# Second-half queries projected beside the first attention and kept in DRAM, in a two-layer hybrid decoder trunk

## The chip, the cores and the metric

The kernel runs on one core of one Trainium2 chip. The metric is the device time of one execution in microseconds, as the median over several runs. All data that the kernel multiplies is float32; each weight and each activation is split into a high part and a remainder, and a product takes three matmuls (high by high, high by low, low by high).

## The reference, cut to what matters

```python
# x: (1, 1024, 1024); layer 0: RG-LRU mixer + MLP; layer 1: sparse attention + MLP
h = rmsnorm(x, norm_mix_g[i]) * (1.0 + sc1) + sh1          # adaLN
# layer 1, token mixer
u = h @ w_in                                               # q, k, v, index q, index k, index weight
q, k, v, qi, ki, wi = jnp.split(u, B_SPLITS, axis=-1)
q = apply_rope(rmsnorm(q.reshape(B, S, 16, 64), q_g), cos, sin)
k = apply_rope(rmsnorm(k, k_g)[:, :, None, :], cos, sin)[:, :, 0]
...
score = einsum("bqh,bqhs->bqs", wib, relu(logits))         # causal, top 256 keys of each query
p = softmax(where(valid, einsum("bqhd,bqkd->bqhk", qb, kg) * 64 ** -0.5, -inf))
out = einsum("bqhk,bqkd->bqhd", p, vg)                     # 16 heads share one key and one value
x = x + g1 * (out @ w_out)
h = rmsnorm(x, norm_ffn_g[i]) * (1.0 + sc2) + sh2
x = x + g2 * (square(relu(h @ ffn_w1[i])) @ ffn_w2[i])
```

## The kernel before, in words

The 1024 positions are two halves of 512. An activation is held as eight tiles of 128 features by 512 positions, so a projection of one half is a run of 128x512 matmuls. Tiles of this size come from one pool of 54 (`tile`, `tileR`); weights pass through `weights`, which loads 512 KB from SP's queue, casts the high part on ScalarE (L322) and subtracts the remainder on GpSimd or VectorE (L328), whose turn is set by the list `lo`. A scheduler decides the final order of the instructions on each engine and their waits.

Layer 1 runs in these stages. First the projections of the first half are made: keys, values and index parts (`kv_steps`, `qi_steps`) and the queries in two groups of 512 columns (`q_group(0, 0)` and `q_group(0, 1)`). A query group is 96 matmuls (L941 to L943), then, for each of four blocks of 128 positions, a root mean square per head, a rotation (`rope`, L804 to L807), a split into high part and remainder (`split_heads`, L859 and L860) and two turns of four 128x128 blocks on TensorE (`turn4`, L868, copied out by ScalarE at L873).

Then comes `attention(0)`, the attention of the first half. It goes through 16 units (a block of positions, a group, a parity), each of four heads: scores on TensorE (L1118, L1119), mask and row minimum on VectorE (L1130), the exponential on ScalarE (L1136), the scaling by the reciprocal sum on GpSimd (L1141), and then per block of keys a transpose (L1146), a copy and a remainder (L1148, L1149) and two matmuls with the values (L1158, L1159). While it runs, `mix` takes pieces from a generator `background()`, at a `rate` of pieces per call: in the first attention the keys, values and index parts of the second half (L819 to L821 by way of `proj_tok`), then the output projection of the first half's group 0 (L345 to L347, added at L1221), which has to wait until nine units are done. `feed` holds back the turns of a step until two later steps are under way.

After it the output projection of group 1, the index scores and the top-k search of the second half, and the MLP of the first half follow (`FFN.single`). Near the end of that MLP the queries of the second half are made. For this the kernel loads the residual `x` of the second half from DRAM (`reload(1)`, L1234), makes the normed input again (`Norm.apply`, L96 to L98; the first one, `hm[1]`, lives only until the first attention) and runs `q_group(1, 0)` and `q_group(1, 1)`, with two of the eight output blocks of the last piece of the MLP between them. Then `attention(1)` runs, with the other six output blocks as the first of its background. Scaling on GpSimd there works on rows of 640 to 1024 elements.

The functions that the change touches, with what calls them:

Of the kernel before, what the change touches and what calls it, by code (L numbers as in the profile page):

```python
# [9 lines left out]
FT = mybir.dt.float32  # L10
# [3 lines left out]
AF = mybir.ActivationFunctionType  # L14
OP = mybir.AluOpType
AX = mybir.AxisListType
# [4 lines left out]
HT = 512  # L21
P = 128
# [3 lines left out]
EPS = 1e-6  # L26
# [21 lines left out]
class Norm:  # L48


    def __init__(self, T, h):
        self.T, self.h = T, h
# [12 lines left out]
    def stat(self, sums=None):  # L65

        T, nc = self.T, self.T.nc
        if sums is None:
            sums = T.ps()[:, 0:4]
            for c in range(4):  # L70
                nc.tensor.matmul(sums[:, c:c + 1], self.acc[:, c * P:(c + 1) * P], T.ones[:, 0:1],
                                 start=True, stop=True)
        r = T.small([P, 4], "rs")
        nc.vector.tensor_scalar(r, sums, 1.0 / D, EPS, op0=OP.mult, op1=OP.add)
        r2 = T.small([P, 4], "rs")
        nc.gpsimd.tensor_tensor(r2, r, T.mhalf, op=OP.pow)
        self.dg = T.nlong()
        for c in range(4):
            nc.vector.tensor_scalar(self.dg[:, c * P:(c + 1) * P], T.ident, r2[:, c:c + 1], None, op0=OP.mult)  # L79
# [117 lines left out]
class Trunk:  # L197
    def __init__(self, ctx, tc, ins, out):
        self.ctx, self.tc, self.nc = ctx, tc, tc.nc
        self.n = 0  # L200
        self.i, self.out = ins, out
        nc = self.nc
        self.const = ctx.enter_context(tc.tile_pool(name="const", bufs=1))
        self.wp = ctx.enter_context(tc.tile_pool(name="wp", bufs=5))
        self.smp = ctx.enter_context(tc.tile_pool(name="smp", bufs=6))
        self.np = ctx.enter_context(tc.tile_pool(name="np", bufs=3))
        self.act = ctx.enter_context(tc.tile_pool(name="act", bufs=54))
        self.pst = ctx.enter_context(ExitStack())
        self.banks(False)
        self.dram = ctx.enter_context(tc.tile_pool(name="dram", bufs=1, space=bass.MemoryType.DRAM))  # L210
        self.tp = None
        self.x, self.xd = {}, {}
        self.parts, self.late = {}, []
        self.fill = []
        self.bg, self.rate, self.due = None, 1, 0.0
        self.lo, self.npump = [1], 1
        self.ada_late, self.loads = [], []
        self.ident = self.const.tile([P, P], FT, name="ident")
        make_identity(nc, self.ident)
        self.identR = self.const.tile([P, P], FR, name="identR")  # L220
        nc.vector.tensor_copy(self.identR, self.ident)
        self.ones = self.const.tile([P, P], FT, name="ones")
        nc.vector.memset(self.ones, 1.0)
        self.mhalf = self.const.tile([P, 4], FT, name="mhalf")
        nc.vector.memset(self.mhalf, -0.5)


# [700 lines left out]
    def q_group(self, h, g, hx, turns):  # L928
# [27 lines left out]
        for t in range(4):  # L956
# [13 lines left out]
            turns.append([lambda p=p, turn=turn: turn(p) for p in range(2)])  # L970
            yield

    def idx_steps(self, t):
        nc, V, A = self.nc, self.nc.vector, self.nc.scalar
        L = (t + 1) * P
# [276 lines left out]
    def run(self):  # L1252
        tc = self.tc
        mod = self.mod = {}
        N = {}
        hm, hf = {}, {}
# [11 lines left out]
        turns = []  # L1268
# [5 lines left out]
        def run(gen):  # L1274
            for _ in gen:
                pass

        def feed(fs, lag=2):
            for f in fs:
                turns.append((yield from f()))  # L1280
                while len(turns) > lag:
                    turn_next()
                yield
# [24 lines left out]
        F = FFN(self, 0, None, hf)  # L1308
        with ExitStack() as st:
# [42 lines left out]
            f2 = F.f2_steps([0], 0)  # L1352
# [23 lines left out]
        with ExitStack() as st:  # L1376
# [47 lines left out]
            def background():  # L1424
                self.second_half()
                yield from feed(self.kv_steps(1, hm[1]), 2)
                yield from feed(self.qi_steps(1, hm[1]), 2)
                self.reload(0)
                while self.units < 8 + 1:
                    yield  # L1430
                yield from self.proj_out(0, mod[1, 2], 0)

            self.banks(True)
            self.bg, self.rate = background(), 1
            self.attention(0)
            self.finish()
            flush()
        with ExitStack() as st:
# [26 lines left out]
            self.lo, self.npump = [1, 1, 0], 2  # L1465
            F = FFN(self, 1, mod[1, 5], hf)
            F.single(0, 0, F.NP - 2)
            self.reload(1)
            hm[2] = N["m1", 1].apply(mod[1, 1], mod[1, 0])
            self.lo = [1, 0]  # L1470
            run(self.q_group(1, 0, hm[2], turns))
            for p in (F.NP - 2, F.NP - 1):
                F.load2(p, 0)
            f2 = F.f2_steps([F.NP - 2, F.NP - 1], 0)
            next(f2), next(f2)
            run(self.q_group(1, 1, hm[2], self.late_turns))
            self.lo = [1]

            def before(u):
                t = u[0]  # L1480
                while len(self.fill) > 36 * (7 - t):
                    self.pump()

            for p in (F.NP - 2, F.NP - 1):
                F.load2(p, 1)

            def background():
                yield from f2
# [4 lines left out]
                yield from self.proj_out(1, mod[1, 2], 0)  # L1493

            self.bg, self.rate = background(), 0.8
            self.banks(False)
            self.attention(1, before)
            self.finish()
            run(self.proj_out(1, mod[1, 2], 1, sqs("f1")))
# [50 lines left out]
```

## Time and profile before

| | us |
|---|---|
| median of 3 runs | 2551.33 |
| lowest, highest | 2551.26, 2557.24 |
| the profiled execution | 2558.93 |
| its span, first to last instruction | 2557.0 |
| TensorE busy in the span | 2435.1 |
| first attention (before its output projection of group 1) | 1333 to 1483 |
| second query stage, to the first scores of the last attention | 1883.7 to 1958.8 |

The profiled execution is 7.6 us over the median of the runs. Its own time is 1.9 us more than its span. A profile lists busy times of each engine: TensorE's matmuls (PE), its weight loads (PEld), VectorE (DVE), ScalarE (ACT), GpSimd (POOL); SP issues most of the transfers. The end of a matmul is modelled: in a row of back-to-back 128x512 matmuls each is listed with some 0.39 us, while one starts every 0.233 us. So a busy share of TensorE says where it stood still, and not how dense the work was.

### The profile page before, as it was taken

The page shows a single profiled execution, that of the slowest core. Times are in us where ns is not written, and L with a number is a line of the kernel's source. Part 1 is how long each engine was busy: PE and PEld are TensorE (multiplying, and loading weights), DVE is VectorE, ACT ScalarE, POOL GpSimd, SP SyncE. Part 2 cuts the span into 40 slices and gives each one's busy share as a digit, 9 for nine tenths or more (in the row PEclk, how much of TensorE's full clock was granted, in tenths as well). Part 3 has the DMA queues.
Part 4 walks back from the last instruction along what each step waited for, and adds up shares of the span by engine and source line. Part 5 has one row for each costly group of instructions (what it writes and reads, how often), then busy time and mean ns, then how long its engine had stood idle before and what let it go on. Part 6 is the DMA issues. An engine that isn't in the chain of part 4 may idle for free. (4 is left out here: it accounts for less than half of the span.)

```text
span 2557.0 us, 30862 instructions
## 1 busy us (share of the span) xinstructions
PE 2435.1 (95%) x10954; PEld 1965.4 (77%) x10954; DVE 1502.1 (59%) x2905; ACT 1227.8 (48%) x2180; POOL 797.6 (31%) x507
## 2 busy tenths in 40 slices
PE   7998999999999999999987999999998999999999
PEld 6776787777788888788776777888887777788887
DVE  5888775788643412566677876555558875321212
ACT  3656465521211233235456667768634974423322
POOL 1000000022221243230238822322326994334442
PEclk8999999999999999999998999999999999999999
DMA  8564675356311577654321522322330114323231
GB/s 262 194 226 167 208 238 188 99 178 222 126 42 42 178 276 269 217 192 177 136 87 42 189 67 67 107 74 91 106 125 1 34 42 140 107 91 99 86 104 58
DMA packets 212284, 342.52 MB, mean 134 GB/s; under 512 B 19658, under 2 KB 123298, under 8 KB 212130
## 3 DMA queue, kind: packets, MB, share of 16 engines
q1 hardware_dynamic: 183184, 295.29, 34.2%
q10 hardware_dynamic: 28946, 45.27, 5.4%
q8 instruction: 86, 1.41, 0.2%
q14 instruction: 68, 0.56, 0.1%
HBM read 274.97 MB, written 65.54 MB: 133 GB/s over the span
## 5 line engine op out<-in xcount | busy, mean ns | idle before, releaser
L328 POOL TENSOR_TENSOR wl<-raw,wh 128x1024 fp32r<-128x1024 f32 (+2 forms) x194 | 470.7, 2433 | 1186.2 <-ACT wh L322 1169.3
L322 ACT CAST wh<-raw 128x1024 fp32r<-128x1024 f32 (+2 forms) x296 | 305.1, 1033 | 615.3 <-PE ps L346 238.8
L345 PE MATMUL ps<-a,wh 128*128 128x512 f32 x1152 | 461.0, 403 | 15.2 <-DVE a L723 7.5
L346 PE MATMUL ps<-a,wh 128*128 128x512 f32 x1152 | 459.2, 399 | 1.5 <-POOL a L1173 1.2
L347 PE MATMUL ps<-a,wl 128*128 128x512 f32 x1152 | 458.2, 399 | 0.7 <-DMA wl<-part 0.7
L345 PE MATMUL pd<-a,wh 128*128 128x512 f32 x1072 | 431.2, 404 | 12.2 <-DVE xc L636 9.4
L347 PE MATMUL pd<-a,wl 128*128 128x512 f32 x1072 | 429.5, 401 | 10.2 <-DVE wl L328 10.2
L346 PE MATMUL pd<-a,wh 128*128 128x512 f32 x1072 | 430.2, 402 | 2.0 <-DVE a L98 2.0
L168 DVE SCALAR_TENSOR_TENSOR a<-ps,mod,a 128x512 f32<-128x512 f32 x352 | 259.7, 746 | 262.8 <-PE ps L347 262.1
L345 PEld LDWEIGHTS ps<-a,wh 128*128 128x128 f32 x1152 | 218.5, 190 | 71.1 <-DVE a L723 7.9
L347 PEld LDWEIGHTS ps<-a,wl 128*128 128x128 f32 x1152 | 218.3, 190 | 54.4 <-DMA wl<-part 1.8
L346 PEld LDWEIGHTS ps<-a,wh 128*128 128x128 f32 x1152 | 218.4, 190 | 54.0 <-POOL a L1173 2.3
L345 PEld LDWEIGHTS pd<-a,wh 128*128 128x128 f32 x1072 | 204.6, 191 | 63.2 <-issue 6.5
L347 PEld LDWEIGHTS pd<-a,wl 128*128 128x128 f32 x1072 | 204.8, 191 | 60.7 <-DVE wl L328 11.1
L346 PEld LDWEIGHTS pd<-a,wh 128*128 128x128 f32 x1072 | 205.3, 191 | 53.2 <-DVE a L98 3.4
L1141 POOL TENSOR_SCALAR s<-s,rr 128x128 f32<-128x128 f32 (+7 forms) x128 | 225.9, 1782 | 35.8 <-DVE rr L1139 25.2
L345 PE MATMUL ps<-hid,wh 128*128 128x512 f32 x512 | 204.9, 400 | 9.6 <-DVE a L168 6.8
L346 PE MATMUL ps<-hid,wh 128*128 128x512 f32 x512 | 203.6, 398 | 0.0
L347 PE MATMUL ps<-hid,wl 128*128 128x512 f32 x512 | 203.6, 398 | 0.0
L1019 ACT ACTIVATE signs<-sc,tc 128x384 int8<-128x384 f32 (+5 forms) x186 | 164.0, 882 | 77.3 <-DVE tc L1034 66.0
L452 DVE SCALAR_TENSOR_TENSOR a<-a,cond,a 128x512 f32<-128x512 f32 x140 | 113.5, 840 | 40.7 <-DMA a<-in_ada_w_dram 40.3
L146 DVE TENSOR_TENSOR a<-r,a 128x512 fp32r<-128x512 f32 x64 | 46.8, 754 | 141.7 <-ACT a L145 140.4
(271 smaller groups left out, 3684.1 us busy)
## 6 DMA issues: line engine op xcount, KB each, us to landing
raw<-in_ffn_w_dram SPq DMA_DIRECT2D x192, 512.0 KB, 3.7
a<-in_ada_w_dram ACTq DMA_DIRECT2D x160, 256.0 KB, 3.4
part<-wl SPq DMA_DIRECT2D x69, 512.0 KB, 3.2
wl<-part SPq DMA_DIRECT2D x69, 512.0 KB, 4.3
part<-wh SPq DMA_DIRECT2D x40, 512.0 KB, 2.8
wh<-part SPq DMA_DIRECT2D x40, 512.0 KB, 3.8
raw<-in_a_w_in_dram SPq DMA_DIRECT2D x34, 512.0 KB, 4.9
raw<-in_a_w_out_dram SPq DMA_DIRECT2D x20, 512.0 KB, 4.1
```

Of the source, the lines that this page charges most:

```text
L146: nc.any.tensor_tensor(ql, r, qh.bitcast(FT), op=OP.subtract)
L168: nc.vector.scalar_tensor_tensor(xt, ps, self.g2[:, m:m + 1], xt, op0=OP.mult, op1=OP.add)
L322: nc.scalar.copy(wh, raw)
L328: eng.tensor_tensor(wl, raw, wh.bitcast(FT), op=OP.subtract)
L345: pe.matmul(out, wh, xh, start=start, stop=False)
L346: pe.matmul(out, wh, xl, start=False, stop=False)
L347: pe.matmul(out, wl, xh, start=False, stop=stop)
L452: nc.vector.scalar_tensor_tensor(a, r, s, a, op0=OP.mult, op1=OP.add)
L1019: A.activation(self.signs[:, 0:L], sc, AF.Sign, bias=0.0 if neg is None else neg.bitcast(FT), accum_out=n)
L1141: G.tensor_scalar(sl[e][:, 0:L], sl[e][:, 0:L], r[:, e:e + 1], None, op0=OP.mult)
```

## The change

The queries of the second half are no longer made near the end of the MLP. A new generator, `q_steps`, makes them a block of 128 positions at a time from `hm[1]`, as a further part of the first attention's background, behind the index parts and ahead of the output projection. Each turned tile goes to DRAM. Where the query stage stood, `load_q` loads the 16 tiles. The reload of `x` for the normed input and the second `Norm.apply` go. The per-head scale is made by one power on GpSimd in place of a Newton iteration on VectorE. The background's rate in the first attention goes from 1 to 1.4, and four output blocks of the MLP's last piece, in place of two, run before the last attention.

```diff
+    def q_steps(self, h, g, hx):
+        def step(t):
+            if not W:
+                W.append(self.b_cols([(512 * g, 512 * g + 512)])[0])
+            ps = yield from self.proj_tok(hx, t, W[0], 512)
+            qf = self.tmp("q")
...
+            A.copy(qf, ps)
+            q2 = self.tile()
+            A.activation(q2, qf, AF.Square)
+            ss, r, rs = (self.small([P, 8], "ssx", 3) for _ in range(3))
+            V.tensor_reduce(ss, q2.rearrange("p (n d) -> p n d", d=64), axis=AX.X, op=OP.add)
+            V.tensor_scalar(r, ss, 1.0 / 64, EPS, op0=OP.mult, op1=OP.add)
+            G.tensor_tensor(rs, r, self.mhalf, op=OP.pow)
+            V.tensor_tensor(q, q, rs.rearrange("p (n o) -> p n o", o=1).to_broadcast([P, 8, 64]), op=OP.mult)
+            r = self.rope(q, ...
+            zs = self.split_heads(r, 8, True)
+            def turn(p):
+                q = self.tileR()
+                self.turn4(zs[p], q)
+                d = self.qd[t, g, p] = self.dram.tile([P, HT], FT, name=self.nm("qd"))
+                nc.sync.dma_start(d, q.bitcast(FT))
...
+    def load_q(self, h):
+        for g in range(2):
+            for t in range(4 * h, 4 * h + 4):
+                for p in range(2):
+                    q = self.qT[t, g, p] = self.tileR()
+                    self.nc.sync.dma_start(q.bitcast(FT), self.qd[t, g, p])
+                    self.turned.add((t, g, p))
...
                 yield from feed(self.qi_steps(1, hm[1]), 2)
+                yield from feed(self.q_steps(1, 0, hm[1]), 2)
+                yield from feed(self.q_steps(1, 1, hm[1]), 2)
                 self.reload(0)
...
-            self.bg, self.rate = background(), 1
+            self.bg, self.rate = background(), 1.4
             self.attention(0)
...
             F.single(0, 0, F.NP - 2)
-            self.reload(1)
-            hm[2] = N["m1", 1].apply(mod[1, 1], mod[1, 0])
-            self.lo = [1, 0]
-            run(self.q_group(1, 0, hm[2], turns))
+            self.load_q(1)
+            self.banks(False)
             for p in (F.NP - 2, F.NP - 1):
-                F.load2(p, 0)
+                F.load2(p, 0), F.load2(p, 1)
             f2 = F.f2_steps([F.NP - 2, F.NP - 1], 0)
-            next(f2), next(f2)
-            run(self.q_group(1, 1, hm[2], self.late_turns))
+            for _ in range(4):
+                next(f2)
```

Lines after the new function are 41 higher in the changed kernel (L1159 is the old L1118).

TensorE inside the first attention, where a unit's transposes, value matmuls and background meet. Before (L819 to L821 are the index projection, L1146 a transpose, L1158 and L1159 the value matmuls):

```order
L1158 MATMUL ps_11958<-nl_11951,Vt 128x512
L1159 MATMUL ps_11958<-pl_11952,Vt 128x512
L819 MATMUL ps_12074<-wh_11623,a_10664 128x384
L820 MATMUL ps_12074<-wl_11624,a_10664 128x384
L821 MATMUL ps_12074<-wh_11623,a_10665 128x384
L1146 MATMUL ps_12083<-ident,s_11814 128x128 x4
L819 MATMUL ps_12074<-wh_11629,a_10682 128x384
```

In the changed kernel (L1187 a transpose; L819 to L821 now the query projection, 512 columns wide):

```order
L1187 MATMUL ps_12613<-ident,s_12305 128x128
L1187 MATMUL ps_12613<-ident,s_12309 128x128
L819 MATMUL ps_12561<-wh_12557,a_10754 128x512
L820 MATMUL ps_12561<-wl_12558,a_10754 128x512
L821 MATMUL ps_12561<-wh_12557,a_10755 128x512
L819 MATMUL ps_12561<-wh_12557,a_10772 128x512
L820 MATMUL ps_12561<-wl_12558,a_10772 128x512
L821 MATMUL ps_12561<-wh_12557,a_10773 128x512
L1199 MATMUL ps_12628<-nl_12570,Vt 128x512
L1200 MATMUL ps_12628<-pl_12571,Vt 128x512
L868 MATMUL ps_12654<-identR,a_12373 128x128 x4
```

Six background matmuls now often stand between a transpose and the value matmuls, where three stood. Between the first scores and the last value matmul the count of `proj_tok` matmuls goes from 192 to 384 and that of the output projection from 96 to 27; the other 69 now stand in one row behind the last value matmul.

VectorE in the changed kernel at the first of the eight query steps (L989 makes the mean square, L991 multiplies the query by the power of it, L1171 is the old L1130):

```order
L989 TENSOR_SCALAR ssx_12107<-ssx_12106 128x8
L991 TENSOR_TENSOR q_12102<-q_12102,ssx_12108 128x512
L1171 ISA s_12159,mn_12156<-ps_12154,cm 128x256
L1171 ISA mn_12156 128x1
L804 TENSOR_TENSOR a_12113<-q_12102,qtab_8239 128x8x32
```

and GpSimd there (L990 is the power between them, L1182 the old L1141):

```order
L1182 TENSOR_SCALAR s_11978<-s_11978,rr_11986 128x256 x2
L328 TENSOR_TENSOR wl_12540<-raw_12537,wh_12539 128x1024
L860 TENSOR_TENSOR a_11996<-a_11475,a_11996 128x4x64
L860 TENSOR_TENSOR a_11999<-a_11475,a_11999 128x4x64
L990 TENSOR_TENSOR ssx_12108<-ssx_12107,mhalf 128x8
L1182 TENSOR_SCALAR s_12159<-s_12159,rr_12167 128x256 x2
```

In seven of the eight steps nothing stands on VectorE between L989 and L991, so it waits there for GpSimd's power, which stands behind GpSimd's other work. Of the added work on GpSimd ten subtractions at L860, six powers and three weight remainders stand ahead of the last scaling of this attention, the rest behind it.

TensorE at the start of the last attention. Before, the last of the output blocks is followed by two turns and then by the scores of four heads in a row:

```order
L346 MATMUL ps_17137<-a_16309,wh_16992 128x512
L347 MATMUL ps_17137<-a_16308,wl_16993 128x512
L868 MATMUL ps_17216<-identR,a_16692 128x128 x4
L868 MATMUL ps_17222<-identR,a_16695 128x128 x4
L1118 MATMUL pd_17028<-a_8232,a_16684 128x512
```

In the changed kernel the scores of a head (four matmuls) come first and the output blocks stand between heads:

```order
L347 MATMUL ps_17118<-a_16876,wl_17067 128x512
L1159 MATMUL pd_17148<-a_8232,a_17016 128x512
L1160 MATMUL pd_17148<-a_8234,a_17016 128x512
L1159 MATMUL pd_17148<-a_10906,a_17016 128x128
L1160 MATMUL pd_17148<-a_10908,a_17016 128x128
L345 MATMUL ps_17161<-a_16793,wh_17060 128x512
L346 MATMUL ps_17161<-a_16794,wh_17060 128x512
```

Ahead of the first transpose of this attention now stand the scores of nine heads and the 48 matmuls of the last four output blocks; the first four blocks stand ahead of the first scores.

## Rows read from the trace of the kernel before

**Rows 1.** The page, busy us, share of the span and instructions of an engine.

```profile
PE 2435.1 (95%) x10954; PEld 1965.4 (77%) x10954; DVE 1502.1 (59%) x2905; ACT 1227.8 (48%) x2180; POOL 797.6 (31%) x507
```

**Rows 2.** Stretches of the span: us, busy us (instructions) of each engine, granted clock, DMA share, GB/s.

```profile
1333.00:1483.00 150.00, 129.47 (x736) 112.60 (x736) 117.92 (x334) 105.81 (x293) 120.78 (x128) 0.91 0.34 118
...
1550.00:1600.00 50.00, 50.00 (x215) 40.18 (x214) 26.86 (x69) 40.60 (x79) 12.82 (x6) 1.00 0.26 85
1883.70:1958.30 74.60, 68.99 (x302) 54.92 (x301) 52.96 (x90) 23.91 (x44) 27.80 (x20) 1.00 0.13 43
1958.00:2107.00 149.00, 138.25 (x797) 112.96 (x798) 121.68 (x271) 122.49 (x252) 141.73 (x83) 0.98 0.09 31
```

**Rows 3.** Waits in 1333 to 1483: engine and line, released by: us, times, longest.

```profile
ACT s L1136 <- DVE mn L1130: 20.6, 14, 7.5
...
DVE kk L897 <- POOL ss L896: 4.5, 4, 2.4
```

**Rows 4.** TensorE in order of time: start us, us, operation, count, idle before.

```profile
1481.58 0.79 PE L868 MATMUL ps<-identR,a 128*128 128x128 f32 x8
...
1883.52 0.39 PE L347 MATMUL ps<-a,wl 128*128 128x512 f32 x1
1883.75 0.39 PE L941 MATMUL ps<-wh,a 128*128 128x512 f32 x1
...
1958.83 0.80 PE L1118 MATMUL pd<-a,a 128*128 128x512 f32 x1
...
1964.72 0.33 PE L1146 MATMUL ps<-ident,s 128*128 128x128 f32 x1 [1.24 <-DVE rr L1139]
```

**Rows 5.** GpSimd in order of time, the first scalings of the last attention.

```profile
1962.77 9.34 POOL L1141 TENSOR_SCALAR s<-s,rr 128x640 f32<-128x640 f32 x5 [3.29 <-PE pd L1119]
```

**Rows 6.** SP's queue in order of time, the reload of x.

```profile
1865.26 3.85 SPq L1234 DMA_DIRECT2D a<-xd  x8
```

**Rows 7.** Transfers by line: count, KB each, median us from issue to landing.

```profile
a<-xd SPq DMA_DIRECT2D x24, 256.0 KB, 5.2
```

**Rows 8.** GpSimd in 1333 to 1483 by line and shape: count, busy us, mean ns, idle before.

```profile
L1141 POOL TENSOR_SCALAR s<-s,rr 128x512 f32<-128x512 f32 x16 | 25.4, 1600 | 8.4 <-PE ps L1146 7.4 <-DVE rr L1139 1.0
...
L328 POOL TENSOR_TENSOR wl<-raw,wh 128x1024 fp32r<-128x1024 f32 x4 | 10.7, 2684 | 4.0 <-ACT wh L322 4.0
...
L860 POOL TENSOR_TENSOR a<-q,a 128x256 fp32r<-128x256 f32 x8 | 5.7, 730 | 0.0
...
L896 POOL TENSOR_TENSOR ss<-ss,mhalf 128x1 f32<-128x1 f32 x4 | 2.3, 576 | 1.8 <-DVE ss L895 1.8
```

**Rows 9.** VectorE in the same stretch, the operations of the queries of the first half.

```profile
L807 DVE TENSOR_TENSOR q<-q,a 128x512 f32<-128x512 f32 x4 | 3.2, 789 | 0.0
...
L804 DVE TENSOR_TENSOR a<-q,qtab 128x256 f32<-128x256 f32 x4 | 2.9, 728 | 0.0
L806 DVE TENSOR_TENSOR q<-q,qtab 128x512 f32<-128x512 f32 x4 | 2.8, 703 | 0.0
L959 DVE TENSOR_TENSOR q<-q,rq 128x512 f32<-128x512 f32 x4 | 2.7, 696 | 0.0
L954 DVE TENSOR_REDUCE ssq<-a 128x8 f32<-128x512 f32 x4 | 2.6, 681 | 5.4 <-ACT a L953 5.4
...
L805 DVE TENSOR_TENSOR a<-q,qtab 128x256 f32<-128x256 f32 x4 | 1.6, 412 | 0.0
```

**Rows 10.** ScalarE in the same stretch.

```profile
L322 ACT CAST wh<-raw 128x1024 fp32r<-128x1024 f32 x9 | 9.5, 1050 | 4.6 <-DMA raw<-in_b_w_out_dram 2.9 <-PE ps L346 1.7
...
L873 ACT CAST a<-ps 128x512 fp32r<-128x512 f32 x15 | 8.2, 589 | 0.7 <-PE ps L868 0.7
...
L859 ACT CAST a<-q 128x256 fp32r<-128x256 f32 x8 | 2.8, 401 | 3.3 <-DVE q L807 3.3
```

More of the change, by code (lines that the diff above doesn't have):

```diff
@@ L75, in stat @@
         r2 = T.small([P, 4], "rs")
-        nc.gpsimd.tensor_tensor(r2, r, T.mhalf, op=OP.pow)
+        nc.gpsimd.tensor_tensor(r2, r, T.mhalf[:, 0:4], op=OP.pow)
         self.dg = T.nlong()
@@ L211, in __init__ @@
         self.tp = None
-        self.x, self.xd = {}, {}
+        self.x, self.xd, self.qd = {}, {}, {}
         self.parts, self.late = {}, []
@@ L223, in __init__ @@
         nc.vector.memset(self.ones, 1.0)
-        self.mhalf = self.const.tile([P, 4], FT, name="mhalf")
+        self.mhalf = self.const.tile([P, 8], FT, name="mhalf")
         nc.vector.memset(self.mhalf, -0.5)
@@ L971, in q_group @@
             yield
+    def q_steps(self, h, g, hx):
+        nc, V, A, G = self.nc, self.nc.vector, self.nc.scalar, self.nc.gpsimd
+        W = []
+        def step(t):
[3 more added lines that the diff above has]
+            qf = self.tmp("q")
+            q = qf.rearrange("p (n d) -> p n d", d=64)
+            A.copy(qf, ps)
[6 more added lines that the diff above has]
+            V.tensor_tensor(q, q, rs.rearrange("p (n o) -> p n o", o=1).to_broadcast([P, 8, 64]), op=OP.mult)
+            r = self.rope(q, self.qtab[0][:, t:t + 1].to_broadcast([P, 8, 64]),
+                          self.qtab[1][:, t:t + 1].to_broadcast([P, 8, 64]), 8)
+            zs = self.split_heads(r, 8, True)
[4 more added lines that the diff above has]
+                nc.sync.dma_start(d, q.bitcast(FT))
+            return [lambda p=p: turn(p) for p in range(2)]
+        return [lambda t=t: step(t) for t in range(4 * h, 4 * h + 4)]
+    def load_q(self, h):
[5 more added lines that the diff above has]
+                    self.turned.add((t, g, p))
     def idx_steps(self, t):
@@ L1482, in before @@
                     self.pump()
-            for p in (F.NP - 2, F.NP - 1):
-                F.load2(p, 1)
             def background():
@@ L1495, in run @@
             self.bg, self.rate = background(), 0.8
-            self.banks(False)
             self.attention(1, before)
```

## The prediction

> **What bounds the kernel now.** I read the page first. TensorE is busy for 95% of the span [rows 1], so a change counts only where it takes work off TensorE's path or fills time in which TensorE stands. The stretches come second [rows 2]. In the middle of the MLP 215 matmuls of 128x512 start in 50 us at the full clock, one every 0.2326 us; that is TensorE's dense price. The first attention is another picture: of 150 us TensorE is idle for 20.5 and its granted clock is 0.91 in the mean, which is 13.5 us more of lost pace, so at most 34 us of slack. No engine is full there: GpSimd 120.8, VectorE 117.9, ScalarE 105.8. The longest waits are handovers around the softmax, such as ScalarE for the row minimum, 20.6 us [rows 3]. The stage is bound by a chain through four engines with GpSimd the busiest. The last attention until 2107 is bound by GpSimd: 141.7 of 149 us. Third, the order of time on TensorE [rows 4]: the second query stage begins at 1883.75, straight behind the MLP, and the first scores of the last attention start at 1958.83.
>
> **Term one: the query stage goes.** From 1883.75 to 1958.83 [rows 4] are 75.1 us, and TensorE is dense there (69.0 of 74.6 us busy at a clock of 1.00 [rows 2]). In it stand 192 query matmuls and the 96 of the MLP's last eight output blocks. Of the latter 48 stay ahead of the first scores: 48 x 0.2326 = 11.2 us. The stage shrinks by 75.1 - 11.2 = **63.9 us**.
>
> What else the old stage did is off the path. The reload, the second normed input, the four casts and remainders of each group, and the rotations lay beside TensorE, and going they give nothing more. The 48 matmuls of the other four output blocks, 11.2 us, move under the last attention. The cover there is GpSimd. Its first five scalings of 640 elements take 9.34 us, 1.87 each, and begin 3.9 us after the first scores [rows 4, 5]. Ahead of the first transpose TensorE now has nine heads of scores, 1280 columns each or 0.58 us at the dense price, and the 11.2 us: 16.4 us (before, four heads took up to 5.9 us there at a slower pace [rows 4]). GpSimd has 9 x 1.87 = 16.8 us for these nine heads and ends them at 3.9 + 16.8 = 20.7, so it isn't starved. The slack of TensorE in this stretch is 10.7 us idle and 0.02 x 149 = 3 us of clock [rows 2], and some 48 turns' blocks of late queries leave it. I cost the move at nothing; with the cover gone it would be 11.2 us.
>
> The loads: eight transfers of x were issued in 3.85 us [rows 6], 0.48 each, and land after 5.2 us [rows 7]. The first query tile needs 0.48 + 5.2 = 5.7 us, all sixteen 16 x 0.48 + 5.2 = 12.9 us, and the first scores need one tile, the next units one each. They stand on SP's queue behind the last MLP weights and ahead of nothing urgent; the reload of x stood in the same place and was issued at 1865.26, 18 us ahead of the old stage. Even if they went out only when the MLP ends, the 11.2 us cover the first tile. Nothing for them, at worst 1.7 us. The sixteen stores of 256 KB wait on SP for ScalarE's copies; ahead of them stand all eight query weights and the first three output weights, so what they hold up is the reload for the first output projection, which now runs later anyway. Nothing.
>
> **Term two: the first attention grows.** TensorE gets 192 matmuls, 192 x 0.2326 = 44.7 us, and 64 turned blocks at 0.79 / 8 = 0.1 us [rows 4], 6.3 us: 51.0 us together. GpSimd gets 16 subtractions of 0.73, eight powers priced as the power there is, 0.58, and five of eight weight remainders of 2.68 [rows 8]: 11.7 + 4.6 + 13.4 = 29.7 us; ahead of the last scaling stand 10, 6 and 3 of them, 18.8 us. VectorE gets eight times 0.68 + 0.70 + 0.73 + 0.41 + 0.70 + 0.79 = 4.0 us [rows 9], 32 us. ScalarE gets eight times two split copies of 0.40 and four of the size of a turn's copy, 0.59, so 3.2 us, and eight casts of 1.05 [rows 10]: 34 us. In exchange 69 matmuls of the output projection, 16.0 us, leave the attention and stand in one dense row behind it, where nothing else runs beside them.
>
> The lower bound: TensorE takes in all 34 us of its slack, so the stage grows by 51.0 - 34 = 17 us. The upper one: nothing is taken in, 51.0 us, and VectorE's eight waits for a power, at 4.5 / 4 = 1.1 us each [rows 3], all add, 9 us: 60 us. Between them I go by the engine that was busiest. GpSimd would have 120.8 + 18.8 = 139.6 us inside the attention; at the share it reached before, 120.8 / 150 = 0.805, that part takes 173.4 us. TensorE has 51.0 - 16.0 = 35 us more in it, so it is no longer slack but still fits: 129.5 + 35 = 164.5 of 173. Behind come the 16.0 us: 189.4, so 39.4 us more than 150. Of the 9 us of waits for powers I add a third, 3 us, since VectorE stood idle for 32 of the 150 us and some of the waits fall there. **42.4 us.**
>
> **The sum.** -63.9 + 42.4 = -21.5 us. The profiled execution would go from 2558.93 to 2537.4. It lies 7.6 us over the median of the runs shown, 2551.33; a difference within the program carries over, so I forecast **2530 us**. By the two bounds of term two alone it would be 2551.3 - 46.9 = 2504 to 2551.3 - 3.9 = 2547.
>
> **Rivals.** *The attention takes the queries for nothing that its slack doesn't cover.* Then the stage grows by 17 us and the kernel takes 2504. For it: TensorE's idle time is there, and a lower clock (0.91) may rise with denser work. Against it: GpSimd, VectorE and ScalarE get some 30 us each as well, and much of the slack lies in the first 50 us, in waits for VectorE. Chance 0.10.
>
> *GpSimd and VectorE work against each other.* The added rotation reads two tiles in each operation. In the rows the same operation at the same shape, 128x256, takes 728 ns at L804 and 412 at L805 [rows 9], so something stretches such operations here. If VectorE's part of a step with two tiles read, 0.70 + 0.73 + 0.41 + 0.70 + 0.79 = 3.3 us, can't run beside GpSimd's, six steps inside the attention add 20 us to GpSimd's 18.8; with 16.0 us of the output projection behind and 6 x 1.1 us of waits the stage grows by 61.4 us, and the kernel takes 2549, no change. Against it: these durations are means from the same mixture of work, and GpSimd's subtraction ran at 0.73 us in it. Chance 0.15. The Trainium skill, page "SBUF — State Buffer", section "Who interferes with whom", says that a VectorE instruction with two inputs in SBUF and a GpSimd instruction that reads SBUF exclude each other, one waiting for the whole length of the other. By that rule this rival is the forecast and the sum is -2.5 us in place of -21.5; the trace agrees in the stretched operation, but no row here shows that whole instructions wait.
>
> *The powers stop VectorE: slower.* Between the mean square (L989) and the product (L991) VectorE has nothing to do in seven of eight steps, and the power stands on GpSimd behind scalings of 1.60 us [rows 8]. Behind VectorE's wait are the row minimum and the remainder of the probabilities, for which ScalarE, GpSimd and TensorE wait in turn. With two scalings ahead, a wait is 2 x 1.60 + 0.58 = 3.8 us. A step costs TensorE 51.0 / 8 = 6.4 us; if nothing hides, it costs 6.4 + 3.8 = 10.2, eight of them 81 us, and the kernel is slower by 17.6: 2569. It decides from 63.9 / 8 = 8.0 us a step on. Against it: the four waits of this kind in the trace took 1.1 us in the mean and 2.4 at most [rows 3]. Chance 0.08.
>
> That the change doesn't do what it says is no rival of weight: the normed input is the same tiles, and the order shows the old stage's matmuls gone.
>
> **How the numbers follow.** 0.3% of the time, 7.7 us, is about what a measurement of this kernel can tell from no change. The forecast has 0.67; its own range is 2504 to 2547, of which some 5% lies within 7.7 us of the old time. Faster: 0.10 + 0.63 + a third of the second rival's 0.15 = 0.78. Same: 0.04 + 0.09 = 0.13. Slower: the third rival and a tail of the second, 0.09. The range 2507 to 2551 leaves out the third rival and most of the first, and takes in the second.
>
> **What would show it.** Right: the first scores of the last attention follow the MLP's last piece after some 11 us; the first attention with its output projection behind takes about 190 us in place of 150, with GpSimd near 0.8 busy in its first 170; the scalings of the last attention begin 4 us after its first scores and follow without gaps. Wrong: waits of VectorE for L990 of over 2 us in the mean; rotations at L804 to L807 well over 0.8 us; a wait of the first scores for a loaded query; a first attention over 214 us, which would eat the whole gain.

## The result, and the profile after

| us | before | after |
|---|---|---|
| median | 2551.33 | 2526.99 |
| lowest, highest of 5 runs | 2550.70, 2557.24 | 2518.77, 2536.51 |
| the profiled execution | 2558.93 | 2526.99 |

The ratio is 0.9898, with a 95% interval of 0.9869 to 0.9927: faster by about 1%, and the median is 3 us from the forecast of 2530. The stages say that it came about in another way than the forecast had it. Busy us of the engines, from the page of the changed kernel (before: [rows 1]):

```profile
PE 2383.0 (94%) x10954; PEld 1960.0 (78%) x10954; DVE 1488.8 (59%) x2872; ACT 1222.7 (48%) x2172; POOL 807.2 (32%) x516
```

TensorE has as many instructions as before and is busy for 52 us less. Stretches of the changed kernel, with the columns of [rows 2]: the middle of the MLP, the first attention up to its last value matmul, and the row of output projection behind it:

```profile
1600.00:1650.00 50.00, 50.00 (x222) 41.42 (x221) 27.57 (x69) 40.76 (x79) 12.41 (x5) 1.00 0.23 77
1309.30:1518.60 209.30, 171.72 (x907) 143.37 (x907) 147.90 (x379) 128.41 (x338) 157.04 (x155) 0.91 0.21 70
1518.60:1537.20 18.60, 18.60 (x93) 15.61 (x92) 9.20 (x12) 7.02 (x15) 2.57 (x6) 1.00 0.86 316
```

The first line is the surprise. The MLP is untouched, the granted clock is 1.00 as it was, and yet 222 matmuls start in 50 us where there were 215 [rows 2]: 0.2252 us apart, not 0.2326. The other two lines hold the second one: attention and row take 227.9 us. TensorE in order of time, at the borders of the stages (first scores; last value matmul; first index scores behind the row; the MLP's last piece and the first scores of the last attention):

```profile
1309.29 0.33 PE L1159 MATMUL ps<-a,a 128*128 128x128 f32 x1 [1.30 <-ACT q L949]
...
1518.60 0.39 PE L1200 MATMUL ps<-pl,Vt 128*128 128x512 f32 x1
...
1537.23 0.39 PE L1028 MATMUL ps<-a,a 128*128 128x512 f32 x1
...
1925.55 0.50 PE L345 MATMUL ps<-a,wh 128*128 128x512 f32 x1 [0.84 <-DVE a L168]
...
1936.38 0.39 PE L347 MATMUL ps<-a,wl 128*128 128x512 f32 x1
1936.60 0.39 PE L1159 MATMUL pd<-a,a 128*128 128x512 f32 x1
```

The first attention begins 24 us earlier than before (1309.3 in place of 1333.4), although no line ahead of it does different work. Not all of that is the pace: in two kernels of the next section that have the old pace it begins at 1323.1 and 1323.8, so some 10 us of the 24 lie within what single executions differ by.

### The profile page after: what moved, and what is told of

It reads as the page before. It is cut to its first block, busy times and chain, and to the rows that moved or that the text cites. A ratio compares the mean times of both kernels' runs of the same rounds, so it can differ in the third digit from the quotient of the medians.

```text
span 2525.2 us, 30881 instructions
## 1 busy us (share of the span) xinstructions
PE 2383.0 (94%) x10954; PEld 1960.0 (78%) x10954; DVE 1488.8 (59%) x2872; ACT 1222.7 (48%) x2172; POOL 807.2 (32%) x516
## 5 line engine op out<-in xcount | busy, mean ns | idle before, releaser
L345 PE MATMUL ps<-a,wh 128*128 128x512 f32 x1152 | 453.6, 396 | 17.9 <-DVE a L723 9.7
L346 PE MATMUL ps<-a,wh 128*128 128x512 f32 x1152 | 451.3, 392 | 0.2 <-DVE a L705 0.2
L347 PE MATMUL ps<-a,wl 128*128 128x512 f32 x1152 | 450.0, 391 | 1.3 <-DMA wl<-part 1.3
L345 PE MATMUL pd<-a,wh 128*128 128x512 f32 x1072 | 423.3, 396 | 13.0 <-DVE xc L636 10.3
L347 PE MATMUL pd<-a,wl 128*128 128x512 f32 x1072 | 421.7, 394 | 10.6 <-DVE wl L328 10.6
L346 PE MATMUL pd<-a,wh 128*128 128x512 f32 x1072 | 422.5, 394 | 2.1 <-DVE a L98 2.1
L1182 POOL TENSOR_SCALAR s<-s,rr 128x128 f32<-128x128 f32 (+7 forms) x128 | 226.1, 1781 | 52.1 <-DVE rr L1180 49.3
L345 PE MATMUL ps<-hid,wh 128*128 128x512 f32 x512 | 202.5, 396 | 13.0 <-DVE a L168 10.7
L346 PE MATMUL ps<-hid,wh 128*128 128x512 f32 x512 | 200.7, 392 | 0.0
L345 PEld LDWEIGHTS ps<-hid,wh 128*128 128x128 f32 x512 | 96.8, 189 | 38.9 <-DVE a L168 13.7
```

The lines of the kernel that those rows point to most:

```text
L345: pe.matmul(out, wh, xh, start=start, stop=False)
L346: pe.matmul(out, wh, xl, start=False, stop=False)
L347: pe.matmul(out, wl, xh, start=False, stop=stop)
L1182: G.tensor_scalar(sl[e][:, 0:L], sl[e][:, 0:L], r[:, e:e + 1], None, op0=OP.mult)
```

## The experiments

**What set the pace?** In the built kernels the three small tiles that `q_steps` adds (32 bytes a partition each) push every pool behind them on. Activation tiles start at 32 modulo 64 bytes before and at 0 after; weight tiles at 0 in both. So the old kernel was padded, and the new one pushed back.

before_pad, the old kernel ahead of `attention(0)`:

```diff
+            for _ in range(3):
+                self.nc.gpsimd.memset(self.small([P, 8], "ssx", 3), 0.0)
```

> The kernel before with one thing added: three small tiles of 32 bytes in the pool of small tiles (each set once by GpSimd), as the change adds them, so that every tile of the pools behind it starts 96 bytes higher: on a multiple of 64 bytes in each partition, as in the changed kernel, where before they start 32 bytes past one. No other instruction changes. Theory A (where tiles start sets the pace of dense matmuls): 222 matmuls of 128x512 start in a dense 50 us, as in the changed kernel's profile, not 215; outside the two stages of the change the changed kernel's profile is some 45 us shorter than the one before, and this kernel gains that: 2551 - 45 = 2506, faster than the changed kernel. Theory B (the pace is that of the chip or of the execution): 215 as before, 2551 within 5 us.

after_shift, the new kernel ahead of `attention(0)`:

```diff
+            self.nc.gpsimd.memset(self.small([P, 8], "pad", 1), 0.0)
```

> The changed kernel with one small tile of 32 bytes more in the same pool, so that the tiles behind it start 32 bytes past a multiple of 64 again, as in the kernel before. Theory A: 215 matmuls in a dense 50 us; the 45 us are lost and the change alone shows: 2527 + 45 = 2572, slower than before by some 20. Theory B: 2527 within 10 us, 222 or 215 as the execution happens to go.

Measured: the padded old kernel 2512.25 us (ratio to before 0.9853, 0.9834 to 0.9872), the new one pushed back 2563.71 (1.0047, 1.0034 to 1.0060). That is theory A, with 39 and 37 us in place of the 45 it named. With equal placement the change is slower: by 14.7 us in the good one (2526.99 against 2512.25, with single runs that overlap), by 0.47% or 12 us in the bad one, where each of its runs is above each of the old kernel's. The pace goes with the placement. First the old kernel in the MLP of layer 0:

```profile
700.00:750.00 50.00, 50.00 (x215) 40.19 (x214) 23.52 (x32) 10.53 (x15) 9.88 (x5) 1.00 0.17 53
```

then the padded old kernel in the same stretch, in its first attention and in its second-half query projection:

```profile
700.00:750.00 50.00, 50.00 (x222) 41.23 (x221) 21.75 (x30) 9.13 (x13) 9.56 (x4) 1.00 0.13 43
1310.80:1458.00 147.20, 128.96 (x728) 111.19 (x728) 118.55 (x332) 104.09 (x289) 120.99 (x128) 0.91 0.34 116
1851.00:1871.00 20.00, 20.00 (x90) 16.57 (x89) 11.48 (x14) 8.27 (x11) 7.13 (x2) 1.00 0.29 99
```

and the new kernel pushed back, in the same stretch of the MLP (216, one more at the edge of the stretch):

```profile
700.00:750.00 50.00, 50.00 (x216) 40.18 (x215) 21.76 (x29) 8.78 (x12) 9.62 (x4) 1.00 0.13 43
```

before_const asks which operand it is. One tile ahead of all others turns the placement round, weights at 32 and activations at 0:

```diff
         make_identity(nc, self.ident)
+        nc.vector.memset(self.const.tile([P, 8], FT, name="pad"), 0.0)
```

> The kernel before with one 32-byte tile ahead of all others, so that weight tiles start at 32 modulo 64 bytes and activation tiles at 0; before it was the other way round, and with the padded kernel both were at 0. If only the start of the activations matters: 2512. If only that of the weights: 2570 to 2590. If a matmul is slow as soon as one of its two operands starts at 32: about 2551, the pace 0.2326 us. If the moving operand alone matters: the MLP at 0.2252 us, the query products at 0.2326.

Measured 2552.23 us, ratio 1.0000 (0.9985 to 1.0016). The middle of its MLP and its query projection:

```profile
1550.00:1600.00 50.00, 50.00 (x215) 40.21 (x214) 27.98 (x91) 38.97 (x77) 11.47 (x6) 1.00 0.28 95
1873.00:1893.00 20.00, 20.00 (x87) 16.08 (x86) 6.41 (x8) 5.39 (x7) 6.01 (x2) 1.00 0.32 107
```

The old kernel, in the query projection:

```profile
1884.00:1904.00 20.00, 20.00 (x87) 16.12 (x86) 6.69 (x8) 5.64 (x6) 6.01 (x2) 1.00 0.32 106
```

With either class of tile at 32 the matmuls are slow, with both at 0 fast. In the MLP the activation is the moving operand and in the query projection the weight is (87 matmuls in 20 us in both mixed kernels, 90 in the padded one); both stages are slow in both mixed kernels, so one operand at 32 is enough, the moving or the other. Only starts of 0 and 32 were tried, and not both at 32.

From here on the padded old kernel is the one to compare with. Its stages and those of the change, from TensorE's order of time in one execution each:

| us | before | padded | change | change less padded |
|---|---|---|---|---|
| to the first scores | 1333.4 | 1310.8 | 1309.3 | -1.5 |
| first attention, to its last value matmul | 147.9 | 147.2 | 209.3 | +62.1 |
| row of output projection behind | 5.6 | 4.8 | 18.6 | +13.8 |
| first index scores to the MLP's norm | 49.4 | 49.8 | 50.7 | +0.9 |
| the norm to the first scores of the last attention | 422.6 | 413.8 | 348.6 | -65.2 |
| last attention | 191.0 | 191.2 | 193.3 | +2.1 |
| the rest, to the end of the span | 407.2 | 393.7 | 395.3 | +1.6 |

The query stage gives 65.2 us, and the first attention with its row takes 75.9. At the old placement the two are much the same: from before to after_shift the one goes from 422.6 to 359.6, the other from 153.5 to 230.2. What are these made of?

**The wait for the power.** Waits in the first attention of the change (columns of [rows 3]):

```profile
ACT s L1177 <- DVE mn L1171: 23.4, 16, 6.4
POOL s L1182 <- DVE rr L1180: 23.0, 9, 9.0
DVE q L991 <- POOL ssx L990: 20.0, 8, 3.2
```

VectorE waits 2.5 us at each of the eight steps. Two kernels take that away. after_no_wait reads the mean square itself:

```diff
-            V.tensor_tensor(q, q, rs.rearrange("p (n o) -> p n o", o=1)...
+            V.tensor_tensor(q, q, r.rearrange("p (n o) -> p n o", o=1)...
```

> The changed kernel with the product on VectorE reading the mean square in place of its power, so that VectorE doesn't wait for GpSimd there; the power is still made. Leaves out the power in the queries of the second half. In the changed kernel these eight waits took 20.0 us in the first attention. Theory W (the waits are what the forecast of the first attention missed): the stage from the first scores to the index scores of the second half goes from 228 to about 208 us, the kernel to 2507. Theory L (the stage is bound by the load of all engines, and a wait taken away comes back elsewhere): under 7 us gained, 2520 or more.

after_rope_first computes the same as the change, with this product behind the rotation:

```diff
-            V.tensor_tensor(q, q, rs.rearrange("p (n o) -> p n o", o=1)...
             r = self.rope(q, ...
+            V.tensor_tensor(q, q, rs.rearrange("p (n o) -> p n o", o=1)...
```

> The changed kernel with the product by the power moved behind the rotation, which commutes with it, so that GpSimd has the rotation's time of some 3 us on VectorE to make the power. Theory W: nearly the whole 20 us of waits go, and the kernel takes 2507 to 2512. Theory L: under 7 us gained.

Measured: 2509.16 us (0.9849, 0.9825 to 0.9873) and 2512.30 us (0.9845, 0.9829 to 0.9862). Attention and row take 216.0 and 217.2 us in place of 227.9, so the wait costs 11 to 12 us of its 20, between the two theories' figures, and it can be hidden at little cost. But with it hidden the change is only as fast as the padded old kernel; 65 us are still paid for the queries. after_rope_first is the base of all that follows. Its attention and row:

```profile
1311.60:1510.20 198.60, 171.13 (x907) 143.26 (x908) 145.25 (x379) 129.09 (x339) 159.31 (x156) 0.91 0.24 79
1510.20:1528.80 18.60, 18.60 (x93) 15.60 (x92) 10.61 (x13) 7.47 (x14) 1.72 (x4) 1.00 0.93 328
```

GpSimd's share is 159.31 / 198.60 = 0.802, just the 0.805 on which term two was built (in the change itself it is 157.04 / 209.30 = 0.750). Is GpSimd then what sets the length? Three kernels each take much of one engine's part of the query steps out. ScalarE's part, 25 us more than in the padded kernel (129.09 against 104.09), is taken out by none.

less_pool has no power and no subtraction; two more copies on ScalarE stand in place of the subtractions:

```diff
-            G.tensor_tensor(rs, r, self.mhalf, op=OP.pow)
...
-            zs = self.split_heads(r, 8, True)
+            zs = []
+            for e in range(2):
+                z = self.tileR()
+                rv = r.rearrange("p (i e) d -> p e i d", e=2)[:, e]
+                for c in range(2):
+                    A.copy(z.rearrange("p (i e) -> p i e", i=4)[:, :, 64 * c:64 * c + 64], rv)
+                zs.append(z)
```

> The kernel with the product behind the rotation, with GpSimd's part of the query steps taken away but for the weight remainders: no power (the product reads the mean square) and no subtraction (ScalarE copies the high part twice). The second-half queries are therefore not the reference's. GpSimd theory (the first attention lasts as long as GpSimd's work divided by the share of 0.80 that it reached before and after): GpSimd's 159.3 us fall by 13.3 and some 12.6 to 133 us, the attention from 198.6 to about 166 us, the kernel from 2512 to about 2480. TensorE theory (its added matmuls stand in rows between the links of the softmax chain and add their length): the attention stays over 190 us and the kernel over 2504.

few_matmuls keeps one of eight slices of the product:

```diff
-        for kt in range(KT):
+        KN = len(hx)
+        for kt in range(KN):
...
-            ps = yield from self.proj_tok(hx, t, W[0], 512)
+            ps = yield from self.proj_tok(hx[0:1], t, W[0], 512)
+            for _ in range(KT - 1):
+                yield
```

> The kernel with the product behind the rotation, with one of the eight slices of each query product kept: 24 matmuls in place of 192 in the first attention, all other work and its pacing as it was. Seven eighths of the second-half query products are left out. TensorE theory: 168 x 0.2252 = 37.8 us leave the attention, 198.6 becomes about 161 us, the kernel about 2474. GpSimd theory: the attention stays near 198 us and the kernel above 2505.

less_vector has no sum of squares, no rotation, no product:

```diff
-            V.tensor_reduce(ss, q2.rearrange("p (n d) -> p n d", d=64), axis=AX.X, op=OP.add)
-            V.tensor_scalar(r, ss, 1.0 / 64, EPS, op0=OP.mult, op1=OP.add)
...
+            V.tensor_scalar(r, q2[:, 0:8], 1.0 / 64, EPS, op0=OP.mult, op1=OP.add)
...
-            V.tensor_tensor(q, q, rs...
-            r = self.rope(q, ...
+            r = q
```

> The kernel with the product behind the rotation, VectorE's part of the query steps taken away but for the mean square of eight values: no sum of squares, no rotation, no product. The second-half queries are therefore not the reference's. VectorE theory (its 145 us in an attention of 198.6 at the share of 0.80 it had in the old one): eight steps less 3.9 us each are 31 us of work less, the attention falls by 30 or more to about 165 us, the kernel to about 2480. Theory of balance (TensorE, VectorE, ScalarE and GpSimd have each taken on 25 to 40 us, so that taking one away leaves the rest; taking away TensorE's or GpSimd's share gave 6 to 8 us): attention 188 to 195 us, kernel 2502 to 2509.

Measured: 2506.65 us (0.9824, 0.9794 to 0.9855), 2503.60 us (0.9802, 0.9773 to 0.9831) and 2496.63 us (0.9777, 0.9759 to 0.9794). The first attention of each, less_pool:

```profile
1312.20:1504.30 192.10, 167.56 (x906) 142.05 (x907) 146.13 (x379) 132.44 (x355) 134.09 (x132) 0.92 0.24 78
```

few_matmuls:

```profile
1312.50:1503.20 190.70, 139.36 (x738) 116.65 (x739) 146.45 (x380) 127.74 (x339) 159.43 (x155) 0.84 0.27 92
```

less_vector:

```profile
1308.00:1490.10 182.10, 164.09 (x906) 140.26 (x907) 118.44 (x333) 129.24 (x340) 154.62 (x156) 0.93 0.25 84
```

Taking 25 us of work from GpSimd shortens the attention by 6.5 us, taking 32 busy us from TensorE by 7.9, taking 27 from VectorE by 16.5. (The median of less_pool lies 6 us below that of after_rope_first, with single runs that overlap; the stage lengths are what is read here.) Both the theory of GpSimd and that of TensorE fall: the first wanted 166 us, the second 161. Nor is VectorE alone the bound, which would have been 165, and the theory of balance wanted 188 to 195 where 182.1 came. VectorE's is the part whose work costs most here, and no single engine's part that was taken out carries the price.

few_matmuls says most about TensorE's idle time. Its attention has 190.70 - 139.36 = 51.3 us of TensorE idle and, at a granted clock of 0.84 (a mean of stretches at 2.4 and at 1.2 GHz), up to 30.5 us of lost pace; after_rope_first has 27.5 and up to 17.9. So the 168 matmuls, 37.8 us at the dense price, went mostly into time in which TensorE stood or ran at the lower clock, and lengthened the attention by only 7.9. Without them 57.3 of the 65.2 us of price remain. They come with the rest of the step; no run adds matmuls alone.

**Does the price come with the number of steps, or with their place?** half makes only group 0 beside the first attention and leaves group 1 where it was:

```diff
-        for g in range(2):
+        for g in range(1):
...
                 yield from feed(self.q_steps(1, 0, hm[1]), 2)
-                yield from feed(self.q_steps(1, 1, hm[1]), 2)
...
-            self.bg, self.rate = background(), 1.4
+            self.bg, self.rate = background(), 1.2
...
+            self.reload(1)
+            hm[2] = N["m1", 1].apply(mod[1, 1], mod[1, 0])
...
             self.load_q(1)
+            run(self.q_group(1, 1, hm[2], self.late_turns))
```

> Only group 0 of the second-half queries is made beside the first attention (product behind the rotation, rate 1.2), group 1 where it was before. If the first attention has slack that the first steps fill before it grows, half the move takes more than half of the gain at less than half of the price: under 2505. If the price is proportional, as much is given back as is saved, and the time stays at 2509 to 2516, like that of the old kernel with padding (2512.25) and of the whole move (2512.3).

Measured 2510.31 us (0.9836, 0.9808 to 0.9863). Attention and row grow by 34.2 us (177.1 and 9.1), and from the MLP's norm to the end of the last attention 33.4 us are saved (366.3 + 205.3 against 413.8 + 191.2). Half the price for half the gain, as the theory of proportion had it: at this rate there is no slack that the first steps have for nothing. (The rate is 1.2 and not 1.4, so the pace of the other pieces changed too.)

rate1, rate2 and rate08 change one number, the rate at which the first attention takes background pieces:

```diff
-            self.bg, self.rate = background(), 1.4
+            self.bg, self.rate = background(), 1
```

> The kernel with the product behind the rotation and the background's rate in the first attention back at 1 in place of 1.4. Before the first query step had reached VectorE the attention was already 13 us later than in the old kernel with padding (96 us in place of 83 at the end of the fourth block's first unit). Rate theory: these 13 us come from the pace of the old background pieces, not from the queries; at rate 1 they go, more of the output projection falls into the dense row behind, at 0.2252 us a matmul, and attention and row together take under 210 us in place of 217, the kernel under 2505. If each piece costs its length wherever it stands: 213 to 221 us together, 2508 to 2516.

> The same kernel at a rate of 2. If background pieces inside the attention fill time in which TensorE stands, pulling the other 69 output-projection matmuls (16 us) into it shortens attention and row together below 213 us and the kernel below 2508. By the rate theory the attention grows by more than the row shrinks: over 221 us together, kernel over 2516.

> The kernel with the product behind the rotation at a rate of 0.8 in the first attention, meant to be the best version. At rates of 2, 1.4 and 1 the attention and the row behind it took 227.6, 217.2 and 211.3 us together, against 152.0 in the old kernel with padding. In the row four query steps stood 7.2 us apart, in the attention 12.5 us. Rate theory: at 0.8 one or two more steps move into the row, each worth some 5 us: 202 to 209 us together, kernel 2498 to 2506, below all others with the whole computation. If rate 1 is the floor, because the attention now idles without pieces: 211 to 216 us, kernel 2508 to 2513.

Measured at 2, 1.4, 1 and 0.8: 2534.73 us (0.9927, 0.9909 to 0.9946), 2512.30 (0.9845, 0.9829 to 0.9862), 2508.24 (0.9820, 0.9802 to 0.9838) and 2515.63 (0.9860, 0.9840 to 0.9880). Attention and row of rate1, where more of the steps stand in the row:

```profile
1305.60:1462.30 156.70, 135.08 (x757) 114.88 (x757) 122.43 (x343) 111.60 (x308) 135.73 (x139) 0.90 0.14 42
1462.30:1516.90 54.60, 51.43 (x241) 42.37 (x242) 31.44 (x49) 22.05 (x43) 26.09 (x22) 0.94 0.67 244
```

Together 227.6, 217.2, 211.3 and 215.1 us from rate 2 down to 0.8. VectorE's sums of squares in rate1, one for each query step:

```profile
1424.97 0.69 DVE L988 TENSOR_REDUCE ssx<-a 128x8 f32<-128x512 f32 x1
1437.33 0.67 DVE L988 TENSOR_REDUCE ssx<-a 128x8 f32<-128x512 f32 x1
1449.66 0.69 DVE L988 TENSOR_REDUCE ssx<-a 128x8 f32<-128x512 f32 x1
1462.20 0.68 DVE L988 TENSOR_REDUCE ssx<-a 128x8 f32<-128x512 f32 x1
1470.90 0.67 DVE L988 TENSOR_REDUCE ssx<-a 128x8 f32<-128x512 f32 x1
1478.12 0.69 DVE L988 TENSOR_REDUCE ssx<-a 128x8 f32<-128x512 f32 x1
1485.36 0.69 DVE L988 TENSOR_REDUCE ssx<-a 128x8 f32<-128x512 f32 x1
1495.66 0.67 DVE L988 TENSOR_REDUCE ssx<-a 128x8 f32<-128x512 f32 x1
```

Inside the attention, until 1462.3, the steps stand 12.3 to 12.5 us apart; in the row behind it 7.2 to 10.3, 8.4 in the mean. That isn't a saving of 4 us a step, since the softmax work of the attention lies between its steps too; attention and row together gain 5.9 us from a rate of 1.4 to 1. The rate theory was right from 2 to 1 in its direction, but rate1 missed both of its figures (211.3 and 2508.24 against under 210 and under 2505), and at 0.8 it is wrong: attention and row grow by 3.8 us, as its rival had it, and the index scores behind take 55.1 us in place of 48.0.

rate2 says less than it seems to. Of the 22 us that it loses to a rate of 1.4, attention and row are 10.4; the last attention takes 200.8 us in place of 192.3. `mix` adds to a count of pieces owed (`due`) at every call, also when the first background has run out, and nothing sets it back, so at this rate the last attention starts with a debt of pieces that it takes in one go. That this is what lengthens it fits, and no run shows it.

The version with the lowest time that computes the whole is rate1. It is clearly faster than before; against the padded old kernel it leads by 4 us, and the two intervals against before overlap. Of the 43 us between before and rate1, 39 are the padding.

## Why the prediction was right, and where it was wrong

**What bounds the kernel** held. TensorE's density decides, as the effect of the pace on the whole shows; but **the dense price** of 0.2326 us, which every term took as a fixed number, moved to 0.2252, and with it 39 us (2551.33 to 2512.25) that stand in no term. The sum took every stretch outside the two stages to stay as it was; that step failed first.

**Term one**, forecast -63.9, measured -65.2 at equal placement. Right, with its details: the first scores follow the MLP's last piece, which begins at 1925.55, after 11.05 us and wait for no load; the 48 moved matmuls cost the last attention 2.1 us in place of nothing. GpSimd starts on its scalings 2.95 us behind the first scores, and its gaps are small:

```profile
1939.55 1.90 POOL L1182 TENSOR_SCALAR s<-s,rr 128x640 f32<-128x640 f32 x1 [12.85 <-DVE rr L1180]
1942.95 3.76 POOL L1182 TENSOR_SCALAR s<-s,rr 128x640 f32<-128x640 f32 x2 [1.50 <-DVE rr L1180]
1947.04 9.35 POOL L1182 TENSOR_SCALAR s<-s,rr 128x640 f32<-128x640 f32 x5 [0.34 <-DVE rr L1180]
```

**Term two**, forecast +42.4, measured +75.9, beyond the upper bound of 60. This is the wrong step, in three parts. First, GpSimd's work in the attention was put too low: 139.6 us, where 157.0 came. The power was priced by a row of the wrong shape, 0.58 us for one column, and the waits by the old ones, 1.1 us. GpSimd's groups in the first attention of the change:

```profile
L328 POOL TENSOR_TENSOR wl<-raw,wh 128x1024 fp32r<-128x1024 f32 x8 | 19.8, 2491 | 0.7 <-ACT wh L322 0.7
L860 POOL TENSOR_TENSOR a<-q,a 128x256 fp32r<-128x256 f32 x23 | 18.7, 827 | 14.2 <-ACT a L859 14.2
...
L990 POOL TENSOR_TENSOR ssx<-ssx,mhalf 128x8 f32<-128x8 f32 x8 | 14.2, 1772 | 4.2 <-DVE ssx L989 4.2
```

With eight columns a power takes 1.77 us, and a row of four columns that points there was at hand in the kernel before, by line (nanoseconds least, median, most):

```profile
L76 POOL TENSOR_TENSOR rs<-rs,mhalf x8: 1006/1038/1494, 14.4 to 2179.9; 128x4 f32<-128x4 f32 x8
```

From 0.576 us for one column [rows 8] and 1.038 for four a line gives 0.154 us a column, and 1.65 us for eight. The waits were 2.5 us each in place of 1.1, and they cost 11 to 12 us in place of 3.

Second, "at the share it reached before" GpSimd was to set the length, 173.4 us. In the change the share was 0.750 and not 0.805; with the wait hidden it came out the same again, 0.802, but not as a cause, since with 25 us less on GpSimd it simply fell to 134.09 / 192.10 = 0.70.

Third, TensorE's added matmuls were to fit beside that ("164.5 of 173"), and what the steps add on VectorE and ScalarE stood in no term of the sum. The 168 matmuls of few_matmuls did fit for the most part, at 7.9 us. But the eight steps cost 65.2 us without the waits, more than TensorE's own part, 192 x 0.2252 + 6.3 = 49.5, and 57.3 of them remain when most of the matmuls are gone. TensorE's idle time and lost pace didn't shrink, as the lower bound supposed; they grew from some 31 us in the padded kernel (147.20 - 128.96, and 0.09 of 147.20) to 45. What was missing, as far as these runs go, is what the steps add to the chain through VectorE, ScalarE and GpSimd: VectorE's part is worth 16.5 us of the 65.2, GpSimd's 6.5. How the rest divides is open, ScalarE's part was not taken out, and that the added work stretches the links of the softmax chain fits all runs but was not shown by itself.

**The rivals.** The first, queries for nothing but 17 us, is out. The second wanted GpSimd and VectorE to exclude each other. The page "SBUF — State Buffer" of the Trainium skill has them do so for whole instructions ("Who interferes with whom"). The trace of the change agrees, in one rotation and the remainder that GpSimd made meanwhile, and then by line (nanoseconds least, median, most):

```profile
1446.48 2.91 DVE L807 TENSOR_TENSOR q<-q,a 128x512 f32<-128x512 f32 x1
...
1446.49 2.34 POOL L328 TENSOR_TENSOR wl<-raw,wh 128x1024 fp32r<-128x1024 f32 x1
...
L807 DVE TENSOR_TENSOR q<-q,a x12: 681/732/2906, 1321.1 to 1516.8; 128x512 f32<-128x512 f32 x12
```

Such a wait stands in VectorE's busy time. With GpSimd idle the rotation at L807 took 0.68 to 0.69 us each time. But the waits are few: all rotations at L804 to L807 for queries and the products at L991 together are some 8 us longer than if each had taken its line's least, an estimate from their durations, where the rival had 20 us for six steps. And VectorE was busy for 145.3 us with GpSimd's full work and for 146.1 with 25 us less of it. So the mechanism is there, and it isn't the price.

The third, powers that stop VectorE, came in part: 2.5 us a wait in place of its 3.8, 11 to 12 us in all, about a third of the 33.5 by which term two was missed. With them the price is 75.9 / 8 = 9.5 us a step, past the 8.0 from which it said that the kernel gets slower; but without them it is 65.2 / 8 = 8.2 already. At equal placement the change is slower by 12 to 15 us. Of the prediction's own signs of being wrong two came: waits for L990 of over 2 us in the mean, and a first attention with its row over 214 us, at 227.9. The rotations took 0.42 to 0.99 us in the mean, and no score waited for a loaded query.

What brought the time back to the forecast was the 39 us of placement, which no term has and which covers the 33.5. That the number was right is luck; the account was wrong.

## What to carry to other kernels

A change that adds a tile moves every tile behind it. Before crediting a change with a gain, look at the pace in a stage that it doesn't touch, and if that moved, time the old kernel with the same tiles added and unused. In a stage that is bound by a chain through four engines, TensorE's idle time took in most of 168 added matmuls, yet the steps that they belong to cost more than TensorE's whole share of them. So sum what a step adds on each engine of the chain, not on the busiest alone, and take the engines' parts out one at a time to see which of them costs. And price a small operation by two rows of its kind with different widths, not by one.

## What was not expected of the hardware

Matmuls of 128x512 started every 0.2252 us (222 in 50 us) when activation and weight tiles both started at 0 modulo 64 bytes, and every 0.2326 us (215) when one of them started at 32, at the same granted clock of 1.00; over the whole kernel that is 39 us of 2551. GpSimd's power took 0.58, 1.04 and 1.77 us for one, four and eight columns. A VectorE operation on two tiles that met a GpSimd operation on two tiles took 2.91 us in place of 0.68, and the trace shows the wait as busy time. And with 168 matmuls out of the first attention the granted clock there was 0.84 in place of 0.91, a larger part at 1.2 GHz; how much of the time saved was lost to that no run separates.
